# One diffusion-backbone layer on one core: the end of the output projection and the start of the up projection put in a new written order, with ScalarE's stores moved to SyncE and the third unit's sums tied to a VectorE instruction

## The chip, the core and the metric

The kernel runs on one core of a Trainium2 chip. A core has a matrix engine (TensorE, PE in the profile), a vector engine (VectorE, DVE), an engine for activation functions, casts and copies (ScalarE, ACT), a general engine (GpSimd, POOL) and SyncE (SP), which here only issues DMA transfers. Each engine works through its own instruction list in order and waits on semaphores for the others. The metric is the device time of one execution in microseconds (us).

## The reference

One layer over 1024 latent tokens of width 1024 and 256 context tokens: modulation, RMSNorm, neighbourhood attention and two-way retention, both merged and projected back, then a gated feed-forward with a depthwise convolution over three neighbouring tokens. The change lies where the first half hands over to the second:

```python
x = x + g1 * _merge(o_na, o_ret, xga, xgb, w_proj_na[l], w_proj_ret[l], w_out[l])
hx2 = _modulate(_rmsnorm(x, norm2_g[l]), sh2, sc2)
x = x + g2 * _conv_ffn(hx2, w_up[l], conv_w[l], conv_b[l], w_down[l])
# _merge ends in   merged @ w_out
# _conv_ffn:  u = h @ w_up;  u = sum(up[:, i:i+n] * conv_w[i]) + conv_b;  (silu(a) * val) @ w_down
```

`w_up` is 1024 x 5632, so `u` has 22 gate and 22 value blocks of 128 columns for 1024 tokens. All of it is fp32.

## The kernel before, in words

**Precision.** An fp32 product is made of three TensorE products. Every operand is split into a high part (a cast on ACT, line 86 of the kernel before) and the rest (a subtraction on DVE, line 87); the three matmuls per block are high x high, high x low and low x high. A tile is called `wc` (split weights), `T` (split activations) and so on, with its two halves. In a product the first two matmuls need only the high part of the weights, and the third needs the low part.

**Output projection.** The 1024 tokens are eight blocks of 128 (`tb` 0 to 7, the last one called `LAST`). For a block `out_mm` multiplies the merged rows by the two halves of `w_out` (24 matmuls each, tile `om`), `out_add` applies the gate and the residual on DVE (tiles `xn`, `x`), `norm_square` and `norm_scale` normalise, `norm_turn` transposes on TensorE (tile `tp`, line 1693), and `norm_rows` writes the modulated rows split into `h2h` and `h2l`, with an unsplit copy `v`. The output rows are stored to DRAM (`d_x`, line 1670).

**Up projection by seven products.** The up projection treats weights and activations as 2 x 2 blocks and makes each pair of output column blocks (a *unit*) from seven products instead of eight (class `Seven`): four of its weight operands are sums S1 to S4 of weight blocks, and four of its activation operands are combinations T1 to T4 of activation blocks. A product is 12 matmuls (four blocks of 128, three matmuls each, 128 x 512) into one 512-wide bank (tile `u`). DVE adds the products to the output blocks `uu` (lines 1403, 1936, 1937, 1941, 1416, 1422; the running sums are `pu`). When all four blocks of a unit are there, `conv` runs: on each of the two 1024-token rows one ACT instruction (line 1884) and two three-operand DVE instructions (lines 1885, 1886; tiles `ta` and `at`), then a silu on ACT (line 1887), the product on DVE (line 1888) and stores.

**The combinations.** Token blocks 4 to 7 give the four parts of each T (`norm_comb`, a DVE subtraction, line 1716). The parts of blocks 4 to 6 go through DRAM: `store_comb` writes them (`d_t`, line 1720, issued on ACT), `comb_raw` reads them back on SP (tile `tr`, line 1772), and `comb_split` casts and subtracts. Those of block 7 go straight from the tiles `v` and `vo`.

**Weights.** For the first two units (the early ones) the sums S1 to S4 were written to DRAM earlier (`d_u`), and are loaded as `ur`. For all later units GpSimd makes them from four loaded blocks (`Seven.load`, lines 1388 to 1391, tiles `s`): S1 = A21 + A22, S2 = S1 - A11, S3 = A11 - A21, S4 = A12 - S2. A later unit's steps (`Seven.step`) are the products A11 x B11, S2 x T2, S1 x T1, S3 x T3, A12 x B21, A22 x T4, S4 x B22.

**What sets the order.** Inside `tc.manual_schedule()` every engine gets its instructions in the order in which the code writes them. Outside of it a scheduler of the framework sets the order. In the kernel before, the manual part ends after the first parts of T2, T3 and T4; the rest of the early units (`open`, which copies a first output block with line 1958, and `close`, which makes the T2, T3 and T4 products), the remaining splits, and the third unit are the scheduler's. `with_vec` makes an instruction wait for the last DVE instruction written before it. It stands in both kernels and is used in this place in the changed one alone.

## Time and profile before

| | us |
|---|---|
| median of 3 runs | 1777.21 |
| the three runs | 1779.65, 1777.21, 1776.79 |
| the profiled execution | 1779.59 |
| its span | 1777.3 |
| TensorE busy in the span | 1721.8 |
| VectorE / ScalarE / GpSimd busy | 1313.6 / 855.7 / 583.4 |
| TensorE busy from 1100 to 1185 us | 69.42 of 85 |
| TensorE busy from 1185 to 1777 us | 579.81 of 592 |

The span is the time from the first to the last instruction that the profile records; the execution's own time is 2.3 us longer. The page is read as follows: an engine's busy time is the sum of its instructions; the idle time in front of an instruction is put down to what released it; a row of a timeline gives start, duration, engine, line, operation, output<-input tiles and, in brackets, that idle time. The granted clock of TensorE (PEclk) is 1.00 at full speed and 0.50 at half.

### The profile page before, as it was taken

How to read it: one execution, taken by the hardware profiler on the slowest of the kernel's cores; microseconds unless marked ns; L12 is line 12 of the kernel's file. 1: busy time of each engine (PE TensorE's matmuls, PEld its weight loads, DVE VectorE, ACT ScalarE, POOL GpSimd, SP SyncE). 2: the span in 40 equal slices, each digit the busy share in tenths (PEclk: the TensorE clock that was granted, in tenths of full speed). 3: DMA queues.
4: the chain of work that ended last, by engine and by line, in shares of the span. 5: the costliest groups of instructions: out<-in, count | busy, mean ns of one | idle time of the engine just before them, and what ended most of it. 6: DMA issues, size and time to landing. Idle time of an engine off the chain costs nothing.

```text
span 1777.3 us, 24675 instructions
## 1 busy us (share of the span) xinstructions
PE 1721.8 (97%) x8333; PEld 1426.0 (80%) x8333; DVE 1313.6 (74%) x2436; ACT 855.7 (48%) x1851; POOL 583.4 (33%) x485
## 2 busy tenths in 40 slices
PE   8799999999999999999999999799999999999997
PEld 3588888888888888788888888577888888788886
DVE  5978888765776766767664567789889999876755
ACT  5667666653443434443443334544444444554444
POOL 2610000002234343565413321245456555211444
PEclk9899999999999999999999999999999999999999
DMA  9133334433231213577668647522322332586753
GB/s 345 53 118 120 114 112 133 139 107 110 72 107 49 72 39 96 175 238 237 203 212 289 207 172 251 190 89 89 116 93 89 113 123 91 166 295 191 240 168 149
DMA packets 142142, 265.27 MB, mean 149 GB/s; under 512 B 16160, under 2 KB 28608, under 8 KB 142016
## 3 DMA queue, kind: packets, MB, share of 16 engines
q1 hardware_dynamic: 120640, 233.29, 40.3%
q10 hardware_dynamic: 21376, 30.42, 4.7%
q8 instruction: 65, 1.06, 0.3%
q14 instruction: 61, 0.50, 0.1%
HBM read 190.49 MB, written 70.53 MB: 147 GB/s over the span
## 4 chain that ended last, share of the span: by engine, by line
PE 42%; issue 6%; DVE 4%; POOL 3%; DMA 1%; ACT 1%; SPq 0%; ACTq 0%; POOLq 0%; DVEq 0%
PE u L1374 27%; PE y L1374 4%; PE pr L112 2%; PE pr L111 2%; PE pr L110 2%; PE om L122 1%; PE om L121 1%; PE om L123 1%; DVE wc L87 1%; POOL x L2043 1%; PE pn L112 1%; PE pn L110 1%; PE pn L111 1%; DVE at L1885 1%; DVE ta L1885 0%
## 5 line engine op out<-in xcount | busy, mean ns | idle before, releaser
L1374 PE MATMUL u<-T,wc 128*128 128x512 f32 x1056 | 253.8, 396 | 12.3 <-ACT uu L1958 4.4
L1374 PEld LDWEIGHTS u<-T,wc 128*128 128x128 f32 x1056 | 200.4, 191 | 60.0 <-ACT uu L1958 5.1
L1374 PE MATMUL y<-wc,ahl 128*128 128x512 f32 x924 | 212.2, 391 | 2.7 <-DVE wc L87 1.8
L1374 PEld LDWEIGHTS y<-wc,ahl 128*128 128x128 f32 x924 | 174.4, 189 | 40.2 <-DVE wc L87 2.5
L87 DVE TENSOR_TENSOR wc<-ur,wc 128x512 fp32r<-128x512 f32 x147 | 133.6, 912 | 64.3 <-ACT wc L86 64.3
L86 ACT CAST wc<-ur 128x512 fp32r<-128x512 f32 x147 | 90.9, 625 | 125.6 <-PE y L1374 72.1
L1374 PE MATMUL u<-h2a,wc 128*128 128x512 f32 x528 | 124.7, 390 | 3.5 <-ACT wc L86 2.0
L111 PE MATMUL mm<-low,wc 128*128 128x512 f32 (+1 forms) x328 | 123.9, 378 | 0.0
L1374 PEld LDWEIGHTS u<-h2a,wc 128*128 128x128 f32 x528 | 98.7, 188 | 25.8 <-ACT wc L86 2.3
L110 PE MATMUL mm<-hx,wc 128*128 128x512 f32 x264 | 107.5, 407 | 0.3 <-DVE vc L221 0.3
L112 PE MATMUL mm<-hx,wc 128*128 128x512 f32 x264 | 105.0, 398 | 0.0
L86 ACT CAST wc<-s 128x512 fp32r<-128x512 f32 x80 | 49.8, 622 | 97.7 <-PE u L1374 93.4
L1513 POOL TENSOR_TENSOR col<-col,bcol 128x32 f32<-128x32 f32 x1 | 0.3, 251 | 282.2 <-DVE aw L538 282.2
L123 PE MATMUL mm<-wc,low 128*128 128x512 f32 (+1 forms) x240 | 91.2, 380 | 0.0
L1374 PE MATMUL u<-hxT,wc 128*128 128x512 f32 x384 | 89.6, 389 | 0.0
L1374 PEld LDWEIGHTS u<-hxT,wc 128*128 128x128 f32 x384 | 72.1, 188 | 14.9
L87 DVE TENSOR_TENSOR wc<-s,wc 128x512 fp32r<-128x512 f32 x80 | 83.2, 1041 | 0.4
L87 DVE TENSOR_TENSOR wc<-raw,wc 128x512 fp32r<-128x512 f32 x88 | 66.0, 759 | 22.3 <-ACT wc L86 22.1
L121 PE MATMUL mm<-wc,hx 128*128 128x512 f32 x192 | 75.2, 392 | 0.6 <-ACT r L1105 0.6
L122 PE MATMUL mm<-wc,hx 128*128 128x512 f32 x192 | 75.2, 392 | 0.0
L1388 POOL TENSOR_TENSOR s<-ur 128x512 f32<-128x512 f32 x20 | 33.5, 1673 | 125.3 <-DVE wc L87 104.5
L87 DVE TENSOR_TENSOR wc<-wr,wc 128x512 fp32r<-128x512 f32 x56 | 55.0, 987 | 22.9 <-ACT wc L86 22.8
(389 smaller groups left out, 4637.9 us busy)
## 6 DMA issues: line engine op xcount, KB each, us to landing
ur<-in_w_up SPq DMA_DIRECT2D x82, 256.0 KB, 2.8
ur<-d_a SPq DMA_DIRECT2D x77, 256.0 KB, 3.0
aw<-in_w_ada SPq DMA_DIRECT2D x32, 512.0 KB, 3.3
pj<-in_w_down SPq DMA_DIRECT2D x44, 256.0 KB, 4.5
d_w<-pj SPq DMA_DIRECT2D x44, 256.0 KB, 2.0
d_a<-sa SPq DMA_DIRECT2D x44, 256.0 KB, 2.0
ur<-d_w SPq DMA_DIRECT2D x44, 256.0 KB, 3.4
d_a<-at SPq DMA_DIRECT2D x33, 256.0 KB, 2.5
```

What stands on the lines that cost most here:

```text
L86: act.copy(hi, src)
L87: (lo_eng or vec).tensor_tensor(lo, src, hi.bitcast(F32), ALU.subtract)
L110: pe.matmul(out, wh, xh, start=k == 0, stop=False)
L111: pe.matmul(out, wh, xl, start=False, stop=False)
L112: pe.matmul(out, wl, xh, start=False, stop=k == n - 1)
L121: pe.matmul(out, ah, bh, start=first, stop=False)
L122: pe.matmul(out, ah, bl, start=False, stop=False)
L123: pe.matmul(out, al, bh, start=False, stop=last)
L1374: pe.matmul(out, a, b, start=first and n == 0, stop=last and n == 2, skip_group_check=True)
L1388: pin(pool.tensor_tensor(self.s1, self.a21, self.a22, ALU.add))
L1885: vec.scalar_tensor_tensor(dst[:, 1:T], u[:, 0 : T - 1], cw[:, blk, 0:1], dst[:, 1:T], ALU.mult, ALU.add)
L2043: pool.tensor_tensor(z, z, fg[:, gs(dh)], ALU.mult)
```

## The change

It rewrites the stretch between the last output-projection block and the third unit, in six parts.

1. The last block's second `out_mm` is written in two halves, with the transposes of the block before between them. `norm_rows` no longer makes half of the `v` copies of two calls on ACT; eight of them (128 x 128) go to DVE. The copy `v` of the last block is now two tiles `vr`.
2. The store of the last output rows (`d_x1`) and the four `d_t` stores of block 6 are issued on SP instead of ACT. On SP, the raw loads of A12 come earlier, the loads of S1, S2 and S3 come after the stores, and the loads of T2 and T3 parts are written in one go.
3. `copy_p1` for the second early unit (an ACT copy that frees its bank for the next product) comes after the first half of the last block's rows.
4. `units[0].open()` and `units[1].open()` come right after the T1 products, ahead of the T2, T3 and T4 splits on ACT.
5. The T2, T3 and T4 products of the early units, the additions and the splits are in the manual part, in this order: unit 0 T2 with its three additions; unit 1 T2; the T3 splits; unit 1's additions; unit 0 T3 and additions; the T4 splits; unit 1 T3; unit 0 T4, with its convolution. `close` is taken in two calls for this. The S3 and A22 weights of the early units are loaded ahead.
6. The third unit's `load` is called with `with_vec`: its first sum waits for the last DVE instruction written before it. The code just before it is `units[0].close(2)`, which ends in the convolution of unit 0.

```diff
-    def out_mm(tb, dh):
+    def out_mm(tb, dh, kbs=range(KB)):
         half, ts = tb // 4, slice((tb % 4) * P, (tb % 4 + 1) * P)
-        m = tok[tb]["m"] = po.tile([P, 512], F32, tag="o", bufs=2, name="om")
-        for kb in range(KB):
+        if 0 in kbs:
...
-        act.dma_start(d_x1[tb * P : (tb + 1) * P], t["x"])
+        if tb < LAST:
+            act.dma_start(d_x1[tb * P : (tb + 1) * P], t["x"])
...
-        act.dma_start(d_t[c, tb - 4], t)
+        (act if tb < LAST - 1 else sync).dma_start(d_t[c, tb - 4], t)
...
-        def close(self, n):
+        def close(self, n, first=True, last=True):
             if n == 0:
-                self.u2, self.u3 = (self.tmp() for _ in range(2))
-                self.prod(self.Y, us[self.n, 1], "T2", True, False)
+                if first and last or not first:
+                    self.u2, self.u3 = (self.tmp() for _ in range(2))
+                    self.prod(self.Y, us[self.n, 1], "T2", True, False)
+                if not first:
+                    return
                 vec.tensor_tensor(self.u2, self.Y, self.p1, ALU.add)
                 vec.tensor_tensor(self.u2, self.W, self.u2, ALU.add)
                 self.add(0, 1, self.Z, self.u2)
             elif n == 1:
-                self.prod(self.Y, ur_load(d_u[self.n, 2]), "T3", False, False)
+                self.prod(self.Y, us[self.n, 2], "T3", False, False)
                 vec.tensor_tensor(self.u3, self.Y, self.p1, ALU.add)
                 self.add(1, 1, self.Z, self.u3)
             else:
-                self.prod(self.Y, ur_load(self.src[1, 1]), "T4", False, True)
+                self.prod(self.Y, a22[self.n], "T4", False, True)
                 self.add(1, 0, self.Y, self.p1)
...
+        out_add(LAST, 0)
+        out_mm(LAST, 1, range(0, KH))
+        norm_turn(LAST - 1, 1)
+        norm_turn(LAST - 1, 0)
+        out_mm(LAST, 1, range(KH, KB))
+        ra = [up_raw(n, 0, 1) for n in range(EARLY)]
+        tr = {(0, b): comb_raw(0, b) for b in range(2)}
+        norm_rows(LAST - 1, 1)
...
+        us = {(n, 3): ur_load(d_u[n, 3]) for n in range(EARLY)}
...
+        sync.dma_start(d_x1[LAST * P : NTB * P], tok[LAST]["x"])
+        cs = {c: norm_comb(LAST - 1, c) for c in (0, 2)}
+        norm_scale(LAST)
+        cs.update({c: norm_comb(LAST - 1, c) for c in (1, 3)})
+        wu[0, "a12"] = w_split(ra[0])
+        wu[1, "a12"] = w_split(ra[1])
...
+        copy_p1(0)
+        for c in range(4):
+            store_comb(LAST - 1, c, cs[c])
+        us.update({(n, c): ur_load(d_u[n, c]) for c in (0, 1, 2) for n in range(EARLY)})
+        a22 = [ur_load(units[n].src[1, 1]) for n in range(EARLY)]
+        op.release()
+        tap = sb("conv", "right")
+        mm_seven(early[0][0][:, 0:512], wu[0, "a12"], h2_rows(KH, 0), False, True)
+        wu[0, "s4"] = w_split(us[0, 3])
+        norm_rows(LAST, 1)
+        copy_p1(1)
+        mm_seven(early[1][0][:, 0:512], wu[1, "a12"], h2_rows(KH, 0), False, True)
+        norm_rows(LAST, 0)
+        tr[0, 2] = comb_raw(0, 2)
+        mm_seven(early[0][1][:, 512:1024], wu[0, "s4"], h2_rows(KH, 1), True, True)
+        wu[1, "s4"] = w_split(us[1, 3])
+        mm_seven(early[1][1][:, 512:1024], wu[1, "s4"], h2_rows(KH, 1), True, True)
+        for b in range(2):
+            comb_split(0, b, tr[0, b])
+        t0 = norm_comb(LAST, 0)
+        wu[0, "s1"] = w_split(us[0, 0])
+        comb_split(0, 2, tr[0, 2])
+        comb_split(0, 3, t0)
+        mm_seven(early[0][1][:, 0:512], wu[0, "s1"], comb_rows("T1"), True, True)
+        tr.update({(c, b): comb_raw(c, b) for c in (1, 2) for b in range(3)})
+        wu[1, "s1"] = w_split(us[1, 0])
+        t2 = norm_comb(LAST, 2)
+        t1 = norm_comb(LAST, 1)
+        mm_seven(early[1][1][:, 0:512], wu[1, "s1"], comb_rows("T1"), True, True)
+        units[0].open()
+        units[1].open()
+        comb_split(1, 3, t1)
         for b in range(3):
-            comb_split(c, b, comb_raw(c, b))
-    for i, n in ((0, 1), (0, 2), (1, 1), (2, -1), (1, 2)):
-        if n >= 0:
-            units[i].close(n)
-        else:
-            units[i].step(0)
+            comb_split(1, b, tr[1, b])
+        t3 = norm_comb(LAST, 3)
+        units[0].close(0)
+        units[1].close(0, first=False)
+        comb_split(2, 3, t2)
+        for b in range(3):
+            comb_split(2, b, tr[2, b])
+        units[1].close(0, last=False)
+        units[0].close(1)
+        tr.update({(3, b): comb_raw(3, b) for b in range(3)})
+        cw = tap.tile([P, 2 * NF, 3], F32, name="cw")
+        sync.dma_start(cw, io["conv_w"])
+        cb = tap.tile([P, 2 * NF], F32, name="cb")
+        sync.dma_start(cb, io["conv_b"])
+        comb_split(3, 3, t3)
+        for b in range(3):
+            comb_split(3, b, tr[3, b])
+        units[1].close(1)
+        units[0].close(2)
+    units[2].load(with_vec)
+    units[2].step(0)
+    units[1].close(2)
...
```

Where the instructions stand, at three places. First VectorE, from the last subtraction ahead of the T2 products on. `T_119..` are the parts of T2 (54/55 before, 44/45 now), T3 (56/57, 46/47) and T4 (58/59, 48/49), `wc<-ur` is the low half of a weight tile, and `pu` and `uu` are the additions. Before:

```order
1706 L1716 TENSOR_TENSOR vo<-vo,v 128x512
1707 L87 TENSOR_TENSOR T_11957<-v,T_11956 128x512
1708 L87 TENSOR_TENSOR wc<-ur,wc 128x512
1709 L87 TENSOR_TENSOR T_11959<-vo,T_11958 128x512
1710 L87 TENSOR_TENSOR wc<-ur,wc 128x512 x2
1711 L1936 TENSOR_TENSOR pu<-u,pu 128x512
1712 L87 TENSOR_TENSOR wc<-ur,wc 128x512
1713 L1937 TENSOR_TENSOR pu<-u,pu 128x512
1714 L1403 TENSOR_TENSOR uu<-u,pu 128x512
1715 L1936 TENSOR_TENSOR pu<-u,pu 128x512
1716 L87 TENSOR_TENSOR wc<-s,wc 128x512
1717 L1937 TENSOR_TENSOR pu<-u,pu 128x512
```

Now:

```order
1722 L87 TENSOR_TENSOR wc<-ur,wc 128x512
1723 L87 TENSOR_TENSOR T_11947<-vr,T_11946 128x512
1724 L87 TENSOR_TENSOR T_11947<-tr,T_11946 128x512 x3
1725 L1875 TENSOR_TENSOR pu<-u,pu 128x512
1726 L1876 TENSOR_TENSOR pu<-u,pu 128x512
1727 L1403 TENSOR_TENSOR uu<-u,pu 128x512
1728 L87 TENSOR_TENSOR wc<-ur,wc 128x512
1729 L1880 TENSOR_TENSOR pu<-u,pu 128x512
1730 L1403 TENSOR_TENSOR uu<-u,pu 128x512
1731 L87 TENSOR_TENSOR T_11949<-vo,T_11948 128x512
1732 L87 TENSOR_TENSOR T_11949<-tr,T_11948 128x512 x3
1733 L87 TENSOR_TENSOR wc<-ur,wc 128x512 x3
```

Before, the low halves of the T2 weights and of several later products stand ahead of the first addition. Now they stand one by one: row 1722 is the low half for unit 1's T2 product, and behind the three additions of that product (1725 to 1727) stands the one for unit 0's T3 product (1728); behind that product's two additions (1729, 1730) and the four T4 splits stands the one for unit 1's T3 product (the first of row 1733). Three additions stand ahead of row 1722 too.

Second, GpSimd where the third unit's sums begin. The first sum's wait on VectorE is reached, by the semaphore's count, with the row `L1824 at<-ta,at` (1743) of the third fence; the trace of the kernel before puts this wait down to a low half of an early weight tile (line 87). The first fence is GpSimd before, the second GpSimd now, the third VectorE now.

```order
301 L1388 TENSOR_TENSOR s<-ur 128x512 [waits DMAHW5_49,DMAHW3_49,DMAHW7_49,DVE_49,PE_49]
302 L1389 TENSOR_TENSOR s<-s,ur 128x512 [waits DMAHW0_49,DMAHW6_49,DVE_49,Pool_49]
303 L1390 TENSOR_TENSOR s<-ur 128x512 [waits DMAHW1_49,DVE_49]
304 L1391 TENSOR_TENSOR s<-ur,s 128x512 [waits DMAHW2_49,PE_49,Pool_49]
305 L1388 TENSOR_TENSOR s<-ur 128x512 [waits DMAHW5_49,DMAHW6_49,DVE_49,Activation_49]
```

```order
301 L1388 TENSOR_TENSOR s<-ur 128x512 [waits DMAHW1_49,DMAHW0_49,DMAHW5_49,DVE_49,PE_49]
302 L1389 TENSOR_TENSOR s<-s,ur 128x512 [waits DMAHW3_49,DMAHW6_49,Activation_49,Pool_49]
303 L1390 TENSOR_TENSOR s<-ur 128x512 [waits DMAHW7_49,Activation_49]
304 L1391 TENSOR_TENSOR s<-ur,s 128x512 [waits PE_49,DMAHW4_49,Activation_49,Pool_49]
305 L1388 TENSOR_TENSOR s<-ur 128x512 [waits DMAHW6_49,DMAHW7_49,PE_49,Pool_49]
```

```order
1737 L1403 TENSOR_TENSOR uu<-u,pu 128x512
1738 L1821 SCALAR_TENSOR_TENSOR ta<-uu,cw,ta 128x1023
1739 L1822 SCALAR_TENSOR_TENSOR ta<-uu,cw,ta 128x1023
1740 L1821 SCALAR_TENSOR_TENSOR at<-uu,cw,at 128x1023
1741 L1403 TENSOR_TENSOR uu<-u,pu 128x512
1742 L1822 SCALAR_TENSOR_TENSOR at<-uu,cw,at 128x1023
1743 L1824 TENSOR_TENSOR at<-ta,at 128x1024
1744 L1821 SCALAR_TENSOR_TENSOR at<-uu,cw,at 128x1023
1745 L1822 SCALAR_TENSOR_TENSOR at<-uu,cw,at 128x1023
1746 L1821 SCALAR_TENSOR_TENSOR ta<-uu,cw,ta 128x1023
1747 L87 TENSOR_TENSOR wc<-s,wc 128x512
1748 L1822 SCALAR_TENSOR_TENSOR ta<-uu,cw,ta 128x1023
```

The sums themselves are the same; the first one now comes after the seven VectorE rows from an addition (line 1403, row 1737) to the product (line 1824). The low half of the third unit's first sum weights (`wc<-s`, 1747) stands behind three more convolution rows.

Third, ScalarE at the end of the output projection, before and now. `d_x_59` and `d_t` are DRAM tensors, `raw` is an A12 weight block.

```order
1189 L1706 ACTIVATE v<-tp_11846,col,a_8902 128x128
1190 L1706 ACTIVATE v<-tp_11851,col,a_8902 128x128 x4
1191 L1669 ACTIVATE xn,ss<-x_11798 128x1024
1192 L1670 DMA d_x_59<-x_11798 128x1024
1193 L1720 DMA d_t<-vo 128x512
1194 L1720 DMA d_t<-v 128x512 x2
1195 L1720 DMA d_t<-vo 128x512
1196 L1787 COPY pu<-u 128x512
1197 L86 CAST wc<-raw 128x512
1198 L1787 COPY pu<-u 128x512
1199 L86 CAST wc<-raw 128x512
```

```order
1183 L1714 ACTIVATE h2h<-tp_11862,col,a_8902 128x128 x3
1184 L1716 ACTIVATE v<-tp_11867,col,a_8902 128x128 x4
1185 L1671 ACTIVATE xn,ss<-x_11798 128x1024
1186 L86 CAST wc<-raw 128x512 x2
1187 L1796 COPY pu<-u 128x512
1188 L86 CAST wc<-ur 128x512
1189 L1714 ACTIVATE h2h<-u,col,a_8902 128x128 x4
1190 L1796 COPY pu<-u 128x512
1191 L1716 ACTIVATE vr<-u,col,a_8902 128x128 x4
```

The five DMA issues stand between the norm's square and the copies and casts before, and are gone from this list now.

## The prediction

> **What bounds the kernel now.** I read the page's first part, then TensorE's waits, then its timeline and clock in the stretch that the change rewrites, and then the engines that release it.

> ```profile
> span 1777.3 us, 24675 instructions
> PE 1721.8 (97%) x8333; PEld 1426.0 (80%) x8333; DVE 1313.6 (74%) x2436; ACT 855.7 (48%) x1851; POOL 583.4 (33%) x485
> ```

> TensorE is the bound, so only its idle time and slow matmuls can be won. In the stretch from 1095 to 1200 us it waits for these (reason, total us, times, longest):

> ```profile
> PE u L1374 <- ACT uu L1958: 4.4, 1, 4.4
> PE u L1374 <- ACT T L86: 3.5, 1, 3.5
> PE u L1374 <- DVE T L87: 3.2, 2, 2.1
> PE u L1374 <- ACT wc L86: 2.0, 1, 2.0
> PE tp L1693 <- DVE v L1708: 1.6, 1, 1.6
> PE u L1374 <- DVE pu L1416: 0.8, 1, 0.8
> ```

> From 1185 us to the end there is next to nothing; the largest is this row of the same view, so what the stretch loses or wins reaches the end undiminished:

> ```profile
> PE y L1374 <- DVE wc L87: 1.8, 2, 1.4
> ```

> TensorE's timeline shows where the gaps lie, and that some groups are slow:

> ```profile
> 1108.86 5.61 PE L1374 MATMUL u<-h2a,wc 128*128 128x512 f32 x24
> 1117.38 6.05 PE L1374 MATMUL u<-h2a,wc 128*128 128x512 f32 x24 [2.04 <-ACT wc L86]
> 1130.16 5.51 PE L1374 MATMUL u<-T,wc 128*128 128x512 f32 x23 [1.07 <-DVE T L87]
> 1140.11 7.16 PE L1374 MATMUL u<-T,wc 128*128 128x512 f32 x24 [4.44 <-ACT uu L1958]
> 1150.75 1.22 PE L1374 MATMUL u<-T,wc 128*128 128x512 f32 x2 [3.48 <-ACT T L86]
> 1154.11 10.83 PE L1374 MATMUL u<-T,wc 128*128 128x512 f32 x34 [2.14 <-DVE T L87]
> 1178.84 3.04 PE L1374 MATMUL u<-T,wc 128*128 128x512 f32 x12 [0.75 <-DVE pu L1416]
> 1185.72 7.87 PE L1374 MATMUL u<-T,wc 128*128 128x512 f32 x34
> ```

> 24 matmuls at 1108.86 take 5.61 us; pipelined, each adds 0.227 us, (7.87 - 0.39)/33 in the last row. The 24 at 1140.11 take 1.55 us more than 5.61, and the 34 at 1154.11 take 2.96 more than the 34 of the last row. The view by stretches says why (after each engine's busy time come the granted clock, the DMA engines' share and GB/s):

> ```profile
> 1145.00:1150.00 5.00, 2.27 (x10) 1.53 (x9) 4.91 (x8) 2.85 (x5) 2.48 (x2) 1.00 0.82 270
> 1150.00:1155.00 5.00, 2.10 (x4) 1.29 (x5) 5.00 (x7) 2.26 (x5) 2.22 (x2) 0.50 0.00 0
> 1155.00:1160.00 5.00, 5.00 (x13) 3.84 (x13) 2.81 (x5) 2.96 (x3) 0.00 (x0) 0.50 0.00 0
> ```

> After the idle 3.48 us the clock stood at 0.50. After 2.04 us idle the 24 matmuls took 0.44 us more than 5.61, so a gap of that size costs little beside itself. Between T1's end (1130.16 + 5.51 - 0.16 of pipeline tail = 1135.5) and 1185.72, TensorE ran 146 matmuls, 33.1 us at full speed, in 50.2 us: 17.1 us were lost, of which 4.5 to the clock.

> **The change, part by part.** *Up to T1 (parts 1 to 3).* ScalarE's list held these issues and then these rows:

> ```profile
> 1112.25 2.86 ACTq L1720 DMA_DIRECT2D d_t<-v  x2
> 1115.21 0.97 ACTq L1720 DMA_DIRECT2D d_t<-vo  x1
> 1116.22 0.58 ACT L1787 COPY pu<-u 128x512 f32<-128x512 f32 x1 [3.87 <-PE u L1693]
> 1102.41 0.41 DVE L1708 TENSOR_SCALAR v<-tp,a,col 128x128 f32<-128x128 f32 x1
> ```

> The copies and casts for A12 no longer wait for these issues, and that pays for the 2.0 us gap. The transposes between the halves hide the 1.6 us wait under 12 matmuls (2.7 us), and GpSimd's sums, gone from here, no longer slow the T1 splits (1.1 us at 1130.16). Against it: the second A12 product must wait for a copy that stands on ScalarE behind another copy, a cast and four row conversions in turn with VectorE's. From the transposes' end near 1113.4 that is 1.1 + 0.5 + 4 x 0.76 + 0.6, to about 1118.5, where the first product ends near 1116.8: 1.7 us; and the first waits 0.7 us for its low weights. The eight `v` conversions cost VectorE 8 x 0.41 = 3.3 us, under TensorE's work but for those four, in a stretch where it was busy half the time. The moved DMA issues stand on SP ahead of later loads; such a load landed in 2.8 us and is wanted later than that:

> ```profile
> 1110.00:1120.00 10.00, 7.96 (x38) 6.18 (x37) 5.44 (x10) 4.93 (x11) 0.55 (x1) 1.00 1.04 398
> ur<-in_w_up SPq DMA_DIRECT2D x82, 256.0 KB, 2.8
> ```

> Were a load late, what T1 gains goes first. Net: 1.6 + 2.0 + 1.1 + 1.1 of slower groups and restarts (0.4 of it the 6.05), less 2.4: **T1 ends 3.4 us earlier**, near 1132.1.

> *The opens (part 4)* take away the 4.4 us gap: the two copies no longer stand behind the T2 to T4 casts.

> *The written order of T2 to T4 (part 5).* A product's third matmul needs the low weights; these stand on VectorE behind the additions of the product before. The rows for the additions and splits:

> ```profile
> 1145.88 0.68 DVE L1937 TENSOR_TENSOR pu<-u,pu 128x512 f32<-128x512 f32 x1
> 1146.60 0.69 DVE L1403 TENSOR_TENSOR uu<-u,pu 128x512 f32<-128x512 f32 x1
> 1147.31 0.69 DVE L1936 TENSOR_TENSOR pu<-u,pu 128x512 f32<-128x512 f32 x1
> 1136.43 1.88 DVE L87 TENSOR_TENSOR T<-tr,T 128x512 fp32r<-128x512 f32 x3
> ```

> A dependent addition takes 0.72 us from start to start, a split 0.61 to 0.68. Unit 1's T2 product: three additions (2.16) + low half (0.7) less the two matmuls that run (0.45) = 2.4 us of wait. Unit 0's T3: the same, 2.4 us; the four T3 splits fit beside it. Unit 1's T3: two additions (1.4), four T4 splits (2.5), low half (0.7), less 0.45 = 4.1 us. Together **8.9 us**. Behind the waiting additions on VectorE stand the next splits, counted here.

> *The tie (part 6).* When unit 0's T4 product ends, VectorE must do an addition, four convolution rows, another addition and a product before GpSimd may begin. The rows, with GpSimd's and a cast's:

> ```profile
> 1176.91 1.27 DVE L1886 SCALAR_TENSOR_TENSOR at<-uu,cw,at 128x1023 f32<-128x1023 f32 x1
> 1173.47 2.32 DVE L1885 SCALAR_TENSOR_TENSOR at<-uu,cw,at 128x1023 f32<-128x1023 f32 x1
> 1178.70 1.21 DVE L1888 TENSOR_TENSOR at<-ta,at 128x1024 f32<-128x1024 f32 x1
> 1172.45 2.26 POOL L1388 TENSOR_TENSOR s<-ur 128x512 f32<-128x512 f32 x1 [20.14 <-DVE wc L87]
> 1124.42 1.62 POOL L1388 TENSOR_TENSOR s<-ur 128x512 f32<-128x512 f32 x1 [11.19 <-DVE wc L87]
> 1126.72 1.64 POOL L1389 TENSOR_TENSOR s<-s,ur 128x512 f32<-128x512 f32 x1 [0.68 <-DVE wc L87]
> 1159.21 0.62 ACT L86 CAST wc<-s 128x512 fp32r<-128x512 f32 x1 [0.93 <-PE u L1374]
> ```

> 0.7 + 4 x 1.2 + 0.7 + 1.2 = 7.4 us to the product's end; S1 and S2, which needs S1, 1.3 to 2.3 each, taken as 3.9 together; the cast 0.6: 11.9 us. TensorE has 16 matmuls meanwhile (four of the third unit's first product, twelve of unit 1's T4), 3.6 us. **It stands 8.2 us** (7.4 to 8.6). Before, the first two sums were made at 1124 and 1126 us, long before use.

> *Behind the tie.* GpSimd then makes eight sums without a pause, and VectorE has unit 1's convolution and the weights' low halves beside it. A convolution row overlapped by a sum takes 2.32 us instead of 1.27; low halves go from 0.68 to these:

> ```profile
> 1180.44 1.77 DVE L87 TENSOR_TENSOR wc<-s,wc 128x512 fp32r<-128x512 f32 x1
> 1182.73 1.18 DVE L87 TENSOR_TENSOR wc<-s,wc 128x512 fp32r<-128x512 f32 x1
> ```

> S2 x T2's third matmul waits for three convolution rows and a low half: 4.3 us alone, 8.2 all slowed, against 5.4 of sums, cast and matmuls: 0 to 2.8, taken 1.7. S3 x T3 waits for a convolution row, two low halves, the product and an addition: 0 to 2.5, taken 1.5. A12's product waits for line 1422 behind five low halves: 0 to 1.7, taken 1.6. **4.8 us** (0 to 7.0); I take the upper half because GpSimd is busy throughout, as in these rows.

> [...]

> *The clock.* Two gaps (4.1 and 8.2 us) are longer than the 3.48 that came before the 0.50 rows. Ten to fourteen matmuls at half speed cost up to 2.3 us behind each; behind the second much of it hides in VectorE's waits. I take **1.5 us**, bounds 0 and 4.5 (what it cost before).

> The sum: 8.9 + 8.2 + 4.8 + 1.5 = 23.4 us lost where 17.1 were, and 3.4 won ahead: +2.9 us. On the profiled execution's 1779.59 us that is 1782.5; its excess over the median is kept out, so the forecast is 1777.2 + 2.9 = **1780.1 us**. Lowest: 8.9 + 7.4 = 16.3, which gives -4.2; highest 8.9 + 8.6 + 7.0 + 4.5 = 29.0, +8.5.

> **The rivals.** *A: the tie costs TensorE nothing*, because the sums still come before they are needed. Then 8.9 + 1.5 = 10.4 are lost: 10.4 - 17.1 - 3.4 = -10.1, 1767 us. For it: GpSimd was early by tens of us before. Against: the first sum's wait now ends with the convolution's product.

> *B: VectorE and GpSimd hardly slow each other, and the clock holds.* Then 17.1 - 17.1 - 3.4 and a little: -4 to 0, 1773 to 1777 us. For it: the row of 1.18; against, the 2.32.

> *C: slower, by the clock.* The place is behind the two long gaps; the price is the 4.5 us that the clock cost before instead of 1.5, so +5.9, 1783 us. It decides once the slow matmuls cost 2.2 us or more in sight. For it: 0.50 for ten us after 3.48 us idle, with 2 matmuls and another gap in between, as here. Against: behind the tie the half-speed matmuls run in VectorE's shadow.

> [...]

> **How the numbers follow.** A time within 0.2% of before (3.6 us) can't be told from no change. The forecast has 0.48 (+0.5 to +5: the same 0.35, slower 0.13), A 0.09 (faster), B 0.15 (the same 0.10, faster 0.05), C 0.28 (slower). Faster 0.14, the same 0.45, slower 0.41. The range leaves out A and the far ends: 1772 (below B's 1773) to 1786 (+8.5). The likeliest case alone is 1778 to 1782.

> **What would show it.** T1's last matmul near 3.4 us earlier than before against the start of the output block; no wait on the copies into `uu` (line 1897 now); three waits of TensorE on line 87 of 2.4, 2.4 and 4.1 us; one wait of about 8 us on ScalarE's cast of S2, with VectorE's line 1824, GpSimd's 1388 and 1389 right ahead of it in the chain of waits; GpSimd empty from 1113 to 1160 us and then busy without a pause; clock rows of 0.50 behind the long waits. The forecast is wrong if the 8 us wait is missing or below 5, if the T2 and T3 products follow without waits, or if new waits appear on loads that SP now issues later.

## The result, and the profile after

The changed kernel took 1792.85 us (median of 4 runs, 1791.04 to 1799.22), the kernel before 1777.0 us beside it: a ratio of 1.0095, 95% interval 1.0067 to 1.0123. Run again later on one chip with the kernel before, it was 1.0102 (1.0088 to 1.0116). It is slower by about 1%, 16 to 18 us; the forecast was 1780.1 us with a range up to 1786. The profiled execution took 1792.47 us. That of the kernel before took 1779.59, which is 2.6 us above its median here, so the two profiles are 13 us apart and not 16.

The page's first lines and TensorE's waits from 1095 to 1230 us, after:

```profile
span 1790.7 us, 24670 instructions
PE 1724.9 (96%) x8333; PEld 1428.3 (80%) x8333; DVE 1322.9 (74%) x2444; ACT 853.9 (48%) x1843; POOL 585.0 (33%) x485
```

```profile
PE u L1374 <- DVE wc L87: 9.6, 5, 4.0
PE u L1374 <- ACT wc L86: 9.2, 1, 9.2
PE u L1374 <- DVE pu L1422: 2.8, 1, 2.8
PE u L1374 <- DVE pu L1416: 2.1, 1, 2.1
PE u L1374 <- ACT pu L1796: 1.8, 1, 1.8
PE u L1703 <- DVE xn L1680: 0.6, 1, 0.6
```

The wait on the copies into `uu` (4.4 us before) is gone, and so is the one on the T3 casts. In their place stand waits on low halves and one of 9.2 us on the cast of the third unit's S2. The rows of TensorE's timeline, after:

```profile
1120.12 3.02 PE L1374 MATMUL u<-h2a,wc 128*128 128x512 f32 x12 [1.80 <-ACT pu L1796]
...
1128.42 8.78 PE L1374 MATMUL u<-T,wc 128*128 128x512 f32 x38
1139.58 4.59 PE L1374 MATMUL u<-T,wc 128*128 128x512 f32 x12 [2.38 <-DVE wc L87]
1146.44 4.61 PE L1374 MATMUL u<-T,wc 128*128 128x512 f32 x12 [2.27 <-DVE wc L87]
1155.03 5.49 PE L1374 MATMUL u<-T,wc 128*128 128x512 f32 x12 [3.98 <-DVE wc L87]
...
1177.60 5.39 PE L1374 MATMUL u<-T,wc 128*128 128x512 f32 x14 [9.15 <-ACT wc L86]
1183.63 2.57 PE L1374 MATMUL u<-T,wc 128*128 128x512 f32 x10 [0.64 <-DVE wc L87]
1188.26 2.98 PE L1374 MATMUL u<-T,wc 128*128 128x512 f32 x12 [2.06 <-DVE pu L1416]
...
1196.71 2.97 PE L1374 MATMUL u<-h2a,wc 128*128 128x512 f32 x12 [2.76 <-DVE pu L1422]
1199.52 8.32 PE L1374 MATMUL u<-T,wc 128*128 128x512 f32 x36
```

The waits are those of the forecast, nearly to the tenth: 2.38, 2.27 and 3.98 us where 2.4, 2.4 and 4.1 stood, 9.15 for 8.2, and 0.64 + 2.06 + 2.76 = 5.5 for 4.8. What was not forecast stands in the second column. Twelve matmuls at full speed take 2.88 us (the T product at 1165.57 us in the same trace); the twelve behind the first three waits took 4.59, 4.61 and 5.49.

To compare versions I use two marks that every trace has: A, the first matmul of the last block's output product, and B, the place in TensorE's list 146 matmuls after T1's end (1185.72 us before; 1199.52 + 2 x 0.227 = 1199.97 after). The starts of A differ between executions by up to 5 us for reasons outside the change, so the distances count:

| version | A | B | A to B | B to the end |
|---|---|---|---|---|
| before | 1095.16 | 1185.72 | 90.56 | 591.6 |
| changed | 1095.61 | 1199.97 | 104.36 | 590.7 |
| changed, second execution | 1098.11 | 1204.98 | 106.87 | 588.5 |

All of the loss lies between the marks. T1 ends 38.25 us after A (1128.42 + 24 x 0.227 = 1133.86), where it ended 40.34 after A before: 2.1 us were won. From there to B it took 66.1 us instead of 50.2. Of these, 33.1 are the 146 matmuls at full speed, 23.2 are waits (8.6 + 9.15 + 5.5), and 8.6 us are slow matmuls (1.7 + 1.7 + 2.6 behind the three waits, 2.05 behind the long one, the rest small); the last 1.1 are matmul tails that each of the seven waits leaves bare (0.39 - 0.227 = 0.16 us each).

### The profile page after: what moved, and what is told of

Same layout as the page of the kernel before. It is cut to its first block, busy times and chain, and to the rows that moved or that the text cites. A ratio compares the mean times of both kernels' runs of the same rounds, so it can differ in the third digit from the quotient of the medians.

```text
span 1790.7 us, 24670 instructions
## 1 busy us (share of the span) xinstructions
PE 1724.9 (96%) x8333; PEld 1428.3 (80%) x8333; DVE 1322.9 (74%) x2444; ACT 853.9 (48%) x1843; POOL 585.0 (33%) x485
## 4 chain that ended last, share of the span: by engine, by line
PE 45%; issue 5%; DVE 4%; POOL 3%; ACT 1%; DMA 0%; POOLq 0%; DVEq 0%; ACTq 0%
PE u L1374 30%; PE y L1374 4%; PE pr L111 2%; PE pr L112 2%; PE pr L110 2%; PE om L123 2%; PE om L122 2%; PE om L121 2%; DVE wc L87 1%; POOL x L2064 1%; PE pn L112 1%; PE pn L110 1%; PE pn L111 1%; POOL pd L2101 0%; DVE at L1821 0%
## 5 line engine op out<-in xcount | busy, mean ns | idle before, releaser
L1374 PE MATMUL u<-T,wc 128*128 128x512 f32 x1056 | 256.9, 400 | 20.7 <-DVE wc L87 9.3
L1374 PEld LDWEIGHTS u<-T,wc 128*128 128x128 f32 x1056 | 201.9, 193 | 69.2 <-DVE wc L87 11.8
L1374 PE MATMUL y<-wc,ahl 128*128 128x512 f32 x924 | 212.3, 392 | 3.1 <-DVE wc L87 1.8
L1374 PEld LDWEIGHTS y<-wc,ahl 128*128 128x128 f32 x924 | 174.5, 189 | 40.5 <-DVE wc L87 2.5
L87 DVE TENSOR_TENSOR wc<-ur,wc 128x512 fp32r<-128x512 f32 x147 | 132.5, 905 | 64.3 <-ACT wc L86 64.3
L86 ACT CAST wc<-ur 128x512 fp32r<-128x512 f32 x147 | 90.9, 622 | 121.2 <-PE y L1374 72.1
L1374 PE MATMUL u<-h2a,wc 128*128 128x512 f32 x528 | 125.2, 392 | 5.7 <-DVE pu L1422 3.5
L1374 PEld LDWEIGHTS u<-h2a,wc 128*128 128x128 f32 x528 | 98.9, 188 | 28.2 <-issue 3.4
L86 ACT CAST wc<-s 128x512 fp32r<-128x512 f32 x80 | 49.7, 622 | 93.8 <-PE u L1374 88.7
L1374 PE MATMUL u<-hxT,wc 128*128 128x512 f32 x384 | 89.8, 390 | 0.0
L87 DVE TENSOR_TENSOR wc<-s,wc 128x512 fp32r<-128x512 f32 x80 | 88.3, 1105 | 0.3
L1374 PEld LDWEIGHTS u<-hxT,wc 128*128 128x128 f32 x384 | 72.0, 188 | 15.2 <-issue 0.3
L87 DVE TENSOR_TENSOR wc<-raw,wc 128x512 fp32r<-128x512 f32 x88 | 67.2, 774 | 21.1 <-ACT wc L86 20.9
L1388 POOL TENSOR_TENSOR s<-ur 128x512 f32<-128x512 f32 x20 | 33.8, 1690 | 143.6 <-DVE wc L87 68.1
L87 DVE TENSOR_TENSOR wc<-wr,wc 128x512 fp32r<-128x512 f32 x56 | 54.6, 979 | 23.1 <-ACT wc L86 22.9
## 6 DMA issues: line engine op xcount, KB each, us to landing
ur<-in_w_up SPq DMA_DIRECT2D x82, 256.0 KB, 2.8
ur<-d_a SPq DMA_DIRECT2D x77, 256.0 KB, 3.0
pj<-in_w_down SPq DMA_DIRECT2D x44, 256.0 KB, 4.7
d_w<-pj SPq DMA_DIRECT2D x44, 256.0 KB, 2.0
d_a<-sa SPq DMA_DIRECT2D x44, 256.0 KB, 2.0
ur<-d_w SPq DMA_DIRECT2D x44, 256.0 KB, 3.5
d_a<-at SPq DMA_DIRECT2D x33, 256.0 KB, 2.6
```

The costliest lines, as they stand in the source:

```text
L86: act.copy(hi, src)
L87: (lo_eng or vec).tensor_tensor(lo, src, hi.bitcast(F32), ALU.subtract)
L1374: pe.matmul(out, a, b, start=first and n == 0, stop=last and n == 2, skip_group_check=True)
L1388: pin(pool.tensor_tensor(self.s1, self.a21, self.a22, ALU.add))
```

## The experiments

One is an edit of the kernel before, one is the changed kernel run again, and all others are edits of the changed kernel. Ratios are to the kernel before, run beside each of them on the same chip. The code is shortened.

### Filled waits: do the slow matmuls come from idle time?

In the three products that wait for a low half, matmuls whose result nobody reads were put between the second and the third matmul, into a bank that had been copied out. What the next text calls the clock's windows are here the pieces of 3.413 us between the changes in the clock records, which the section after this one shows.

```diff
+                if k == 0 and fill:
+                    pe.matmul(bank, wh, xh, ...); pe.matmul(bank, wh, xl, ...)
+                    for _ in range(fill):           # 9, 9 and 16
+                        pe.matmul(units[0].X, wh, xh, start=True, stop=True)
+                    pe.matmul(bank, wl, xh, ...)
```

> Changed kernel with 9, 9 and 16 matmuls more, whose results nobody reads, put into the three waits for low halves in the T2 and T3 products; nothing else differs. Theory (the slow groups come from TensorE's idle time within the clock's windows): the clock stays at 1.00 from 1130 us to the tie's wait, the waits in front of the third matmuls shrink to 0.1 to 0.4 us, the products end no later, and 1.7 + 1.7 + 2.6 = 6.0 us come back: 1787 us. Rival (the slow groups have another cause than idle time): 1793 us or more, with the same slow groups.

Measured: 1787.54 us, ratio 1.0043 (1.0028 to 1.0058), where the changed kernel had 1.0095 and 1.0102. TensorE's timeline of this kernel (line 1405 holds the fillers, 1406 the product's third matmul, 1374 its remaining ones):

```profile
1137.94 2.35 PE L1405 MATMUL u<-T,wc 128*128 128x512 f32 x9 [0.33 <-DVE pu L1883]
1140.13 0.39 PE L1406 MATMUL u<-T,wc 128*128 128x512 f32 x1
1140.36 2.23 PE L1374 MATMUL u<-T,wc 128*128 128x512 f32 x9
...
1145.76 2.23 PE L1374 MATMUL u<-T,wc 128*128 128x512 f32 x9
...
1152.84 2.68 PE L1374 MATMUL u<-T,wc 128*128 128x512 f32 x11
...
1172.53 8.83 PE L1374 MATMUL u<-T,wc 128*128 128x512 f32 x24 [9.15 <-ACT wc L86]
```

Nine matmuls take 2.23 us, full speed, and the third matmuls wait no more than 0.35 us. The kernel does 34 matmuls more and is faster by half a percent: the slow groups came from idle time. The gain in the ratio, 9 to 10 us, is more than the 6.0 expected. Between the marks the profiled execution, the slowest of its four runs, won only 3.9 us on the first profile of the changed kernel and 6.4 on the second; behind the long wait its slow group was longer than in the first (24 matmuls in 8.83 us). Where the rest of the gain lies, the profile does not show.

### The changed kernel again: is the cost fixed?

> The changed kernel itself once more, on the chip and with the runs of the kernel before that the next kernel is compared with. Theory (where TensorE's idle stretches fall on the clock's windows differs from execution to execution, and with it what they cost): 1.007 to 1.012 of the kernel before, 1791 to 1800 us, a wider spread than that of the kernel before; the waits on the low halves and on the cast of S2 within 0.2 us of the first profile, the slow groups not. Rival (the cost is fixed): the same groups of matmuls slow by the same amounts.

Measured: 1798.16 us (1795.93 to 1799.75), ratio 1.0102 (1.0088 to 1.0116). The waits came out as before (1.81, 2.38, 2.37, 4.06, 9.15 us). The slow groups did not. This row follows the same 1.8 us wait that left the clock alone in the first execution:

```profile
1122.60 4.61 PE L1374 MATMUL u<-h2a,wc 128*128 128x512 f32 x12 [1.81 <-ACT pu L1796]
```

The view by stretches, cut into pieces of 3.4 us, shows where the difference lies. After each stretch comes its length, TensorE's busy time first, and the clock third from the right. The changed kernel, first execution:

```profile
1116.55:1119.95 3.40, 1.77 (x8) 1.13 (x6) 2.69 (x8) 1.73 (x4) 0.00 (x0) 1.00 0.98 327
1119.95:1123.35 3.40, 3.23 (x14) 2.70 (x15) 1.71 (x5) 3.40 (x9) 0.00 (x0) 1.00 1.01 371
...
1136.95:1140.35 3.40, 1.02 (x5) 0.67 (x4) 3.33 (x6) 0.00 (x0) 0.00 (x0) 0.99 0.00 0
1140.35:1143.75 3.40, 3.40 (x9) 2.63 (x8) 1.68 (x4) 0.83 (x2) 0.00 (x0) 0.51 0.58 180
1143.75:1147.15 3.40, 1.13 (x5) 0.63 (x4) 2.57 (x4) 2.48 (x5) 0.00 (x0) 1.00 0.26 78
1147.15:1150.55 3.40, 3.40 (x10) 2.62 (x9) 0.00 (x1) 1.75 (x3) 0.00 (x0) 0.50 0.00 0
1150.55:1153.95 3.40, 0.50 (x2) 0.06 (x1) 3.37 (x6) 0.00 (x0) 0.00 (x0) 1.00 0.00 0
1153.95:1157.35 3.40, 2.33 (x6) 1.85 (x7) 2.23 (x4) 0.00 (x0) 0.00 (x0) 0.50 0.00 0
1157.35:1160.75 3.40, 3.40 (x10) 2.63 (x9) 1.02 (x2) 0.00 (x0) 0.00 (x0) 0.50 0.00 0
```

The second execution, and the kernel before around its 2.04 us gap:

```profile
1119.55:1122.95 3.40, 1.59 (x7) 0.99 (x6) 2.54 (x8) 2.26 (x6) 0.00 (x0) 0.99 0.92 310
1122.95:1126.35 3.40, 3.40 (x10) 2.67 (x9) 1.86 (x4) 3.06 (x7) 0.00 (x0) 0.51 1.04 395
```

```profile
1112.65:1116.05 3.40, 2.69 (x16) 2.08 (x15) 0.75 (x1) 0.00 (x0) 0.55 (x1) 1.00 1.03 406
1116.05:1119.45 3.40, 2.07 (x8) 1.40 (x9) 1.78 (x3) 3.23 (x8) 0.00 (x0) 1.00 1.06 407
```

The clock changes within 0.1 us of the borders of these pieces: in the clock records of two traces, of the kernel before and of the changed kernel's first execution, all changes lie on a grid of 3.413 us, to within 0.01 us. In these rows a piece at full clock with 1.59 us or less of busy TensorE is followed by one at half clock; one with 1.77 or 2.07 is not. That does not hold everywhere: later in the first execution, with 1.53 us of work, the clock stayed:

```profile
1184.67:1188.08 3.41, 1.53 (x7) 0.94 (x5) 3.41 (x4) 1.76 (x3) 3.41 (x3) 1.00 0.05 13
1188.08:1191.50 3.42, 3.24 (x14) 2.74 (x15) 3.42 (x4) 0.22 (x1) 3.34 (x3) 1.00 0.86 327
```

Cut at the exact borders, the same two traces hold 1006 pieces at full clock from 10 to 1770 us. All 16 with up to 1.48 us of busy TensorE were followed by half clock, and none of the 990 with 1.53 us or more; in the second execution, above, one with 1.59 us was. The 2.04 us gap of the kernel before was cut in two by a border; the 2.3 us gaps now fell each into one piece. Which waits are followed by slow matmuls differs between the two executions: the slow groups cost 8.6 us in the first one and about 12 in the second (1.6 + 1.6 + 1.6 + 2.4 + 3.4 + 1.6). The wider spread that was expected is not shown: here the runs of this kernel spread over 3.8 us (4 runs) and those of the kernel before over 5.9 (15), the first time over 8.2 and 4.8 (4 runs each).

### The order on VectorE alone, with the tie kept

The weights of the next product and the splits of the next combination are written ahead of the additions; the third unit's sums still wait for the convolution.

```diff
-        units[0].close(0)
-        units[1].close(0, first=False)
-        comb_split(2, 3, t2) ...            # then additions, product, additions, T4 splits
+        wprep(0, 0); units[0].mul(0); wprep(1, 0); units[1].mul(0); wprep(0, 1)
+        comb_split(2, ...)                  # T3
+        units[0].sums(0); wprep(1, 1); units[0].mul(1); units[1].sums(0); units[1].mul(1)
+        wprep(0, 2)
+        comb_split(3, ...)                  # T4
+        units[0].sums(1); wprep(1, 2); units[0].mul(2); units[1].sums(1); units[0].sums(2)
```

Here `wprep` splits a weight tile, `mul` makes the product and `sums` its additions.

> Changed kernel with the tie kept, but on VectorE and ScalarE the weights of the next product and the splits of the next combination stand ahead of the additions that wait for a product. Theory (three waits, 2.38 + 2.27 + 3.98 = 8.6 us, and the half clock that follows them, about 6 us): 14.6 us less than the changed kernel, about 1778 us, and the clock at 1.00 up to the tie's wait, which stays at 8 to 9 us. Rival (the chain through the tie sets the end, and it starts no earlier): 1786 us or more, with a longer wait at the tie.

Measured: 1778.27 us, ratio 0.9994 (0.9984 to 1.0003). The theory held, with a gain of some 18 us where it had 14.6. TensorE's timeline:

```profile
1130.61 16.48 PE L1374 MATMUL u<-T,wc 128*128 128x512 f32 x72
1148.11 3.00 PE L1374 MATMUL u<-T,wc 128*128 128x512 f32 x12 [1.01 <-DVE pu L1884]
...
1162.90 2.08 PE L1374 MATMUL u<-T,wc 128*128 128x512 f32 x4 [6.35 <-ACT wc L86]
1169.43 6.48 PE L1374 MATMUL u<-T,wc 128*128 128x512 f32 x20 [4.45 <-DVE wc L87]
```

T1, T2 and T3 run as 72 matmuls without a gap at full speed. The wait on the cast of S2 is still there, 6.35 us, and behind it now one of 4.45 us on its low half. This order alone gives back the whole loss, 1.0% or some 18 us: the three waits (a new one of 1.0 us on an addition stands in their place), their slow matmuls, and a little of the tie's stretch.

### The tie moved, and the tie taken out

First the sum waits for the last T4 split instead of the convolution's product:

```diff
+        mark = <last VectorE instruction, taken right after the T4 splits>
-    units[2].load(with_vec)
+    units[2].load(with_split)               # waits for mark
```

> Changed kernel, only the tie's other end differs: the third unit's first sum waits for the last split of T4 instead of the product of unit 0's convolution. Theory (the tie costs the wait on the cast of S2, 9.15 us, the three waits behind it, 0.64 + 2.06 + 2.76 = 5.5 us, and about 2 us of half clock behind the long wait): these 16.7 us come back, so about 1776 us where the changed kernel has 1792.9, with waits of 2.4, 2.3 and 4.0 us ahead unchanged. Rival (VectorE's convolution and low halves are the bound there whoever starts the sums): the wait on the cast goes, the others grow, 1784 us or more.

Measured: 1784.5 us, ratio 1.0030 (1.0019 to 1.0041): the rival's number. The wait on the cast of S2 is gone, but the eight sums now meet the low halves for T4, and unit 0's T4 product waits for one of them; VectorE's and TensorE's rows:

```profile
1157.99 4.05 DVE L87 TENSOR_TENSOR wc<-ur,wc 128x512 fp32r<-128x512 f32 x3
```

```profile
1168.86 2.60 PE L1374 MATMUL u<-T,wc 128*128 128x512 f32 x10 [2.30 <-DVE wc L87]
```

Then no tie at all:

```diff
-    units[2].load(with_vec)
+    units[2].load()
```

> Changed kernel with nothing but the tie taken out: the third unit's sums start when their weights have landed. Theory (the tie costs what tying to the last T4 split gave back, 8 us, and as sums near 1128 us meet VectorE where it later waits for products, some more): 1.001 to 1.004 of the kernel before, 1780 to 1786 us; the waits of 2.4, 2.3 and 4.0 us stay. Rival (the tie is the whole loss): 0.998 or less.

Measured: 1783.99 us, ratio 1.0022 (1.0013 to 1.0031), on the chip where the changed kernel had 1798.16: the tie is worth 14 us. The theory's number held, though the gain is more than the 8 us that it started from; of the three waits the 4.0 came apart into 2.5 and 0.8 us. The tie is not the whole loss.

### Both together

> Both together: the early weights and splits, and the sums tied to the last T4 split. Theory: the two gains add, 16.7 + 14.6 less up to 5 us that VectorE gives back behind T4, 1762 to 1767 us, faster than the kernel before. Rival (VectorE's work in the stretch is the bound once TensorE no longer waits for the sums): 1772 us or more.

Early weights and splits with the tie at the last T4 split: 1776.27 us, ratio 0.9977 (0.9967 to 0.9987). It is faster than the kernel before, but by 4 us, not by 10 or more: the rival. A to B it takes 80.66 us, 9.9 less than before; from B to the end 597.0, 5.4 more. Where it is given back, TensorE waits for an addition, and ahead of that VectorE's low halves take 1.7 us each while GpSimd works without a pause (1173.06 to 1186.25 us):

```profile
1197.17 5.46 PE L1374 MATMUL u<-h2a,wc 128*128 128x512 f32 x12 [4.03 <-DVE pu L1423]
```

```profile
1178.22 5.17 DVE L87 TENSOR_TENSOR wc<-s,wc 128x512 fp32r<-128x512 f32 x3
```

Without any tie, the rest alike:

> The version with early weights, without any tie: the third unit's sums start when their weights have landed, near 1128 us. Theory (VectorE and GpSimd slow each other by the same sum wherever they meet): within 1.5 us of the version tied to the last T4 split, 1775 to 1778 us, with VectorE's T2 and T3 splits at 1.2 to 1.8 us. Rival (early sums delay the splits that TensorE waits for, and with the half clock cost more): 1780 us or more.

1773.6 us, ratio 0.9972 (0.9962 to 0.9982): the same as tied to the split, within the intervals, as the theory said, if a little under its numbers. A to B 78.89 us, B to the end 596.1.

### Is it VectorE's own work, or GpSimd's?

From the version with the tie at the split, the third, fourth and fifth units' sums are left out; their products take raw weight blocks, so the output is not the reference's.

```diff
+            if hasattr(self, "j") and self.n in (2, 3, 4):
+                self.s1, self.s2, self.s3, self.s4 = self.a21, self.a22, self.a11, self.a12
+                return
```

> The version with early weights and the tie at the last T4 split, without the sums of the third, fourth and fifth unit: their products take the loaded weight blocks themselves, so the output differs from the reference. Theory (behind T4 VectorE is held by GpSimd's sums, about 1 us a row, and this gives the 5 us back): VectorE's convolution rows at 1.3 us and low halves at 0.7 us, waits on lines 1417 and 1423 mostly gone, 1768 to 1771 us. Rival (VectorE's own work is the bound): 1775 us or more.

Measured: 1768.14 us, ratio 0.9936 (0.9913 to 0.9959). A to B 74.88 us, B to the end 592.55: the 5 us behind B are no longer lost. Up to 1167 us GpSimd runs nothing in this stretch and VectorE's rows take their short times, as this one of the first convolution, which took 2.31 us in the version with the sums (line 1822, at 1159.35 us):

```profile
1153.59 1.27 DVE L1825 SCALAR_TENSOR_TENSOR at<-uu,cw,at 128x1023 f32<-128x1023 f32 x1
```

So what held VectorE behind T4 was in good part GpSimd's sums. The wait for the addition of line 1417 is gone, and the 4.03 us for that of line 1423 shrink to 2.24. A wait of 3.1 us ahead of T4 stays, where it was 1.8 with the sums. GpSimd has no part in it: VectorE works through its own list, in which it waits 1.5 us for casts of ScalarE.

### Up to T1

Two moves ahead of T1 were added to the version with the tie at the split: the second unit's copy right behind the first's, and two of block 6's subtractions behind the row conversions.

```diff
         copy_p1(0)
+        copy_p1(1)
...
         norm_rows(LAST, 1)
-        copy_p1(1)
+        for c in (1, 3):
+            store_comb(LAST - 1, c, norm_comb(LAST - 1, c))
```

> The version with early weights and the tie at the last T4 split, and ahead of it two moves: the second unit's copy of its first product right behind the first unit's, and two of block 6's subtractions behind the last block's first row conversions. Theory (the changed kernel's 1.8 us wait on that copy, and half of the 1.3 us that T1 missed against the forecast, come from these places): T1 ends 2 to 3 us earlier, and because VectorE's list starts earlier too, 1.5 to 2.5 us of it reach the end, 1774 us. Rival (VectorE's backlog behind T4 sets the end): the waits behind T4 grow by as much, 1776 us or more.

1774.71 us, ratio 0.9979 (0.9965 to 0.9992), against 0.9977 without the moves. The copy's wait is gone (24 matmuls for A12 in 5.72 us), but T1 ends only 0.8 us earlier against A, because its first matmul now waits 1.2 us for a cast. A to B is 80.68 us, as it was: the wait on line 1417 grew from 2.58 to 4.21 us. The rival's mechanism was right, VectorE's backlog takes what was won; its 1776 us were not reached.

Next, the kernel before with one part of the change alone, the stores on SP (and the A12 loads ahead of them):

```diff
-        act.dma_start(d_t[c, tb - 4], t)
+        (act if tb < LAST - 1 else sync).dma_start(d_t[c, tb - 4], t)
```

> Kernel before, with the last output rows' store and the four stores of block 6's combinations issued on SP, and the raw A12 loads moved ahead of them; all else as before. Theory (ScalarE's five issues make the 2.0 us wait before the A12 products): this wait is gone or under 0.5 us, and 1.5 to 2 us reach the end, 1775.5 us. Rival (the T1 splits on VectorE stand ready no earlier): the 1.1 us wait before T1 grows to 2 or 3 us, 1777 us.

1773.71 us, ratio 0.9972 (0.9960 to 0.9984): 5 us, more than the 2 expected. TensorE's timeline:

```profile
1113.16 5.70 PE L1374 MATMUL u<-h2a,wc 128*128 128x512 f32 x24
...
1124.14 5.60 PE L1374 MATMUL u<-T,wc 128*128 128x512 f32 x24
1131.57 5.74 PE L1374 MATMUL u<-T,wc 128*128 128x512 f32 x24 [1.82 <-ACT uu L1960]
1145.91 1.22 PE L1374 MATMUL u<-T,wc 128*128 128x512 f32 x2 [8.60 <-ACT T L86]
```

There is no wait before A12 and none before T1, which ends 36.25 us after A instead of 40.34, better than in the changed kernel. GpSimd's first sum starts only at 1127 us here, behind the T1 splits. The wait for the `uu` copies shrinks from 4.44 to 1.82 us; part of the gain is lost to a longer wait on the T3 casts (8.60 us instead of 3.48), ahead of which ScalarE waits 3.8 us for the load of `conv_b` and then for T3 parts that are read back.

### All that paid

Early weights and splits, no tie, the two moves, and the eight `v` copies back on ScalarE (`norm_rows(..., True)` in both places):

> All that has paid so far: early weights and splits, no tie, the second unit's copy right behind the first unit's, two of block 6's subtractions later, and the eight `v` copies back on ScalarE. Theory (VectorE is the bound from T2 on, so what leaves its list, 8 x 0.41 us, and what starts it earlier reaches the end): 2 to 4 us less than the version with early weights and no tie, 1770 to 1772 us. Rival (the waits behind T4 on lines 1417 and 1423 take it back): 1773.5 us or more.

1771.23 us, ratio 0.9950 (0.9936 to 0.9963): **0.5% faster than the kernel before**, the best of the versions that compute the reference. Its mechanism is not shown: T1 ends 2.1 us earlier against A than without the moves and copies (36.15 instead of 38.29), but A to B is 78.63 us, only 0.3 less, and the waits ahead of T4 and behind it, 3.5 and 4.1 us, are as long as there. The ratio's further 0.2% was also measured on another chip. The same rear part behind the front order of the kernel before:

> Early weights and splits, no tie, and up to T1 the order of the kernel before with the stores on SP (the version that took 4 us less up to T1's end than the kernel before), save that the transposes stand between the halves of the output product. Theory (that order reaches T1's end earliest, and nothing behind it differs): 1769.5 to 1772 us, at or under the other version of this call. Rival (T1's splits wait for the blocks read back, which SP now loads behind the stores): no better than 1773.5 us.

1774.37 us, ratio 0.9967 (0.9955 to 0.9978). Its T1 waits are under 0.5 us each, so the rival's mechanism is not what was seen; it waits 4.9 us for the addition ahead of T4 where the other waits 3.5 us. In both, this product goes on 54.7 to 54.9 us after A, so what comes before it only shifts TensorE's wait. Both still wait there, on VectorE (TensorE's waits, best version):

```profile
PE u L1374 <- DVE pu L1423: 4.1, 1, 4.1
PE u L1374 <- DVE pu L1884: 3.5, 1, 3.5
```

## Why the prediction was wrong

**The waits behind the written order: right.** 8.9 us forecast, 8.6 measured, each wait in its place; their cause, the low halves behind the additions, is confirmed by the version that moves them (72 matmuls without a gap).

**The tie: right in place, a little small.** 8.2 forecast, 9.15 measured. The chain to the product's end was 7.5 us where 7.4 stood; the first two sums took 2.18 + 2.12 us, not 3.9 together, while a convolution row of the other unit stood beside both:

```profile
1172.52 2.18 POOL L1388 TENSOR_TENSOR s<-ur 128x512 f32<-128x512 f32 x1 [59.54 <-DVE at L1824]
1174.78 2.12 POOL L1389 TENSOR_TENSOR s<-s,ur 128x512 f32<-128x512 f32 x1
1173.61 2.17 DVE L1822 SCALAR_TENSOR_TENSOR at<-uu,cw,at 128x1023 f32<-128x1023 f32 x1
```

**Behind the tie: right.** 4.8 forecast, 5.5 measured, with VectorE's rows slowed as quoted in the forecast (2.17 to 2.31 us for the rows of the convolution, 1.4 to 1.8 for the low halves).

**Up to T1: half.** 3.4 forecast, 2.1 measured. The output product's part came out (1.8 us). But the four row conversions that the second A12 product's copy stands behind began late: VectorE had two subtractions and three low halves ahead of its half of the first one, and ScalarE waited for it. ScalarE's row:

```profile
1117.26 0.46 ACT L1714 ACTIVATE h2h<-u,col,a 128x128 fp32r<-128x128 f32 x1 [2.28 <-DVE vr L1718]
```

I had counted the conversions, not what stands in front of them on the other engine.

**The clock: the step that failed.** "Two gaps (4.1 and 8.2 us) are longer than the 3.48 that came before the 0.50 rows. [...] I take 1.5 us, bounds 0 and 4.5 (what it cost before)." It cost 8.6 us in the first execution and about 12 in the second. I took the length of a gap as what decides, and read from the 2.04 us gap before that short gaps are harmless. That gap had been cut by the border of two 3.4 us pieces. What the traces show ahead of half clock is little work in such a piece: three gaps of 2.3, 2.3 and 4.0 us, each with at most 1.1 us of work in its piece, were each followed by a slow group. The upper bound was wrong by the same error: it was the cost of two slow groups before, where six gaps now offered themselves. Its arithmetic for one group was off as well: ten to fourteen matmuls at half speed cost 2.3 to 3.2 us more (0.227 each), not up to 2.3. But the groups here cost 1.7 to 2.6; what counted was how many there were.

With 8.6 us for the clock, 2.1 for the front and the measured waits, the sum gives 23.2 + 8.6 + 1.1 - 17.1 - 2.1 = +13.7 us, which is the difference between the marks (104.36 - 90.56 = 13.8). The 1.1 are the bare tails of the matmuls, which the forecast left out. Of the 10.9 us between forecast and marks, the clock makes 7.1, the waits 1.3, the front 1.3 and the tails 1.1.

**The rivals.** C named the right mechanism and the wrong place and price: it put the slow matmuls behind the two long gaps alone and capped them at 4.5 us. A (the tie costs nothing) fell: taking it out is worth 14 us. B (VectorE and GpSimd hardly slow each other) fell with the rows above and with the version without sums.

**What the forecast's sum does not tell** is what undoing the two costs is worth. In the changed kernel they add up, as forecast, but undoing the written order gives back 18 us and undoing the tie 14, but both together 23, not 32: with neither, TensorE waits for VectorE, slowed by GpSimd, behind T4.

## What to carry to other kernels

In a written order, put what the next product needs (the low half of its weights, the next split) ahead of the additions that wait for the product before; a short in-order wait on VectorE can be paid twice, as TensorE's idle time and as matmuls at half clock behind it (here 2.38 us and 1.7 us more). When pricing gaps, lay them over the pieces that the clock records show (3.413 us here) and ask how much work is left in each; here two gaps of 2.38 and 2.27 us cost 1.7 us each in slow matmuls, together more than the 2.6 us behind one of 3.98. Where the borders of the pieces fell differed between two executions, so the price is a range (8.6 and about 12 us). Tie an instruction to the last row that it must not disturb, not to whatever was written last: here that was the end of a convolution, 7.5 us later. Leaving the tie out did as well (1.0022 against 1.0030, and 0.9972 against 0.9977).
